# Dilated attention: splitting q and k in the tokens' layout and turning them in the transfer that turns the probabilities

## The chip, the cores and the metric

The kernel runs on one core of a Trainium2 chip. The metric is the device time of one execution in microseconds (us); of several executions the median is given. All times of rows are counted from the start of the profiled span. Engines are named as in the profile: PE (matrix multiply; PEld is its weight load), DVE (vector), ACT (scalar, activations), POOL (GpSimd), SP (the engine that here only issues transfers).

## The reference, cut to what matters

Two encoder layers over 1024 tokens of width 1024. Layer 0 mixes tokens by latent attention, layer 1 by dilated sliding-window attention in three groups; each layer ends in a squared-ReLU MLP. The change touches only the attention of layer 1:

```python
DIL_GROUPS = ((128, 1), (512, 4), (2048, 16))      # window, dilation
DIL_HEADS, DIL_HEAD_DIM = 16, 64
proj = (h @ w_in).reshape(B, S, 3, 3, 16, 64)       # group, (q k v), head, width
for gi, (window, dilation) in enumerate(DIL_GROUPS):
    q = rms_norm(proj[:, :, gi, 0], g_q[gi])
    k = rms_norm(proj[:, :, gi, 1], g_k[gi])
    v = proj[:, :, gi, 2]
    # query i sees keys i + j*dilation, |j| <= window/(2*dilation) = 64 (group 2: 64 tokens of a residue)
    s = q k^T * 64**-0.5 + bias(rel. position);  lse = logsumexp(s);  p = exp(s - lse);  o = p v
# the three groups' o are merged by softmax over their lse, then o @ w_o
```

## The kernel before

The program has two copies of the computation, one in halves (each number as a sum of two 16-bit floats, `self.half` true) and a slower one that runs only if a check of ranges fails. Only the first runs here.

The dilated stage is the method `dil`. Its work is cut into 96 steps `("qk", g, pr, tp)`: group `g` (0 to 2), pair of heads `pr` (0 to 7), and pair of 128-token tiles `tp` (0 to 3). A unit is one `(g, pr)`, four steps. Six empty steps end the stage. The loop over steps writes the instructions of several steps interleaved:

- `attend(ready, ...)` at the top: for the two query tiles `t` that are ready, `products` multiplies q with a span of 256 keys (three half products, hi*hi, lo*hi, hi*lo, and two heads that lie on the partitions 0 to 63 and 64 to 127, so 6 matmuls a tile, L2345); `scores` adds the bias and takes the maximum on DVE (L2366) and the exponential on ACT (L2372). The probabilities are split into halves `ph` (ACT L2409, then the remainder on DVE or POOL, L2410) and one transfer issued by SP turns all 128x128 blocks of `ph` into `pT` (L2411): 16 blocks a step in groups 0 and 1, 8 in group 2.
- `project` for the first and the second token tile of the step (L532 to L534, 24 matmuls of 256 columns each), which give q and k of two heads, 512 columns for 128 tokens: `psproj`.
- between the two: `stacks` for the q and k that were made two steps earlier. Four PE transposes (L2316) turn `qn`, tokens by features, into `psq`, features by tokens; ACT copies it to a half `hi` (L2321) and DVE makes the remainder `lo` (L2322). They land in `kT`, one tile of a unit with room for all 1024 keys and the q of four tiles. The tiles of this step are then `ready` for the next.
- `emit`, and `av` for the tiles whose `pT` was made by the step before: 8 matmuls a tile in groups 0 and 1, 4 in group 2 (L2424, L2425), summed by DVE (L2432).
- `qkstep` at the end, on what was just projected: squares (ACT L2295), sums (DVE L2296), the reciprocal root (ACT L132, L133, DVE L134 to L136), `qn` = projection times root (DVE L2305), and the gain on the q half (POOL L2307).

So q and k projected in step m are turned in step m+2 and used by `products` in step m+3; probabilities made in step n are used by `av` near the end of step n+1.

The PE's order is that of the program text (`pin_from`); the other engines' orders are set when the program is built, by a scheduler that lays the instructions out in modelled time. Each engine and each queue then runs in its order. SP issues, beside the turning transfers, the loads of weights (`wqkr`), of values (`vraw`), of the bias (`bt`), and the stores of `U`.

Of the kernel before, what the change touches and what calls it, by code (L numbers as in the profile page):

```python
# [9 lines left out]
F32 = mybir.dt.float32  # L10
F32R = mybir.dt.float32r
F16 = mybir.dt.float16
BF16 = mybir.dt.bfloat16
I32 = mybir.dt.int32
AF = mybir.ActivationFunctionType
ALU = mybir.AluOpType
# [4 lines left out]
P = 128  # L21
D = 1024
S = 1024
# [18 lines left out]
class K:  # L42
# [108 lines left out]
    def parts(self, hi, lo, src, scale=1.0, check=True):  # L151

        if not self.half:
            return self.split(hi, lo, src)
        nc = self.nc
        nc.scalar.activation(hi, src, AF.Copy, scale=scale)  # L156
        if not check:
            return nc.vector.scalar_tensor_tensor(lo, src, scale, hi, op0=ALU.mult, op1=ALU.subtract)
        self.nseen += 1
        assert self.nseen <= self.seen.shape[1]  # L160
        return nc.vector.scalar_tensor_tensor(lo, src, scale, hi, op0=ALU.mult, op1=ALU.subtract,  # L161
                                              accum_out=self.seen[:, self.nseen - 1 : self.nseen])
# [2028 lines left out]
    def dil(self, at0, at1, tail, wqk, vd):  # L2191


        nc, a, tc = self.nc, self.a, self.tc
# [5 lines left out]
        D_ = lambda name, shape, dt, bufs: dpool.tile(list(shape), dt, tag=name, bufs=bufs, name=self.nm(name))  # L2200
# [88 lines left out]
        def qkstep(u, tp, ps):  # L2289

            g = u["g"]
            p8 = ps.rearrange("p (n e) -> p n e", e=64)
            sq = self.T("dsq")
            ms = self.sm("dms", 8)
            nc.scalar.activation(sq, ps, AF.Square, scale=0.125)  # L2295
            nc.vector.tensor_reduce(ms, sq.rearrange("p (n e) -> p n e", e=64), op=ALU.add, axis=AX.X)  # L2296
            r = self.rstd(ms, 8, "dr", self.half)
            if self.half:
                y4 = self.sm("y4", 8)
                nc.gpsimd.tensor_tensor(y4, r, r, op=ALU.mult)  # L2300
                nc.gpsimd.tensor_tensor(y4, y4, y4, op=ALU.mult)  # L2301
                nc.gpsimd.tensor_tensor(most, most, y4, op=ALU.add)
            qn = self.T("qn")
            q8 = qn.rearrange("p (n e) -> p n e", e=64)
            nc.vector.tensor_tensor(q8, p8, r.unsqueeze(2).broadcast_to([P, 8, 64]), op=ALU.mult)  # L2305
            qq = qn.rearrange("p (i n e) -> p i n e", i=2, e=64)[:, :, 0:2, :]
            nc.gpsimd.tensor_tensor(qq, qq, gain[:, g : g + 1, :].unsqueeze(1).broadcast_to([P, 2, 2, 64]), op=ALU.mult)  # L2307
            return qn

        def stacks(u, tp, qn):  # L2310

            ps = PS("psq")
            for k in range(2):
                for i in range(2):
                    c = i * 256 + (1 - k) * P
                    nc.tensor.transpose(ps[:, (2 * k + i) * P : (2 * k + i + 1) * P], qn[:, c : c + P], self.ident)  # L2316
            s1 = 4 + tp % 2
            hi, lo = (u["k"][:, k, :].rearrange("p (s x) -> p s x", x=256)[:, tp : s1 + 1 : s1 - tp, :] for k in range(2))
            x = ps.rearrange("p (k x) -> p k x", k=2)
            if self.half:  # L2320
                nc.scalar.activation(hi, x, AF.Copy, scale=64.0)  # L2321
                nc.vector.scalar_tensor_tensor(lo, x, 64.0, hi, op0=ALU.mult, op1=ALU.subtract)  # L2322
            else:
                nc.scalar.activation(hi, x, AF.Copy)
                nc.vector.tensor_tensor(lo, x, hi.bitcast(F32), op=ALU.subtract)
            for i in range(2):
                c = S + (tp % 2 * 2 + i) * P
                u["q"][2 * tp + i] = u["k"][:, :, c : c + P]
# [7 lines left out]
        def window(g, t):  # L2336
            return t // 2 * 256 if g == 2 else min(max(P * t - 64, 0), S - 256)

        def products(u, t, pss, i):
            w0 = window(u["g"], t)  # L2340
            q = u["q"].pop(t)
            for n, (a, b) in enumerate(((0, 0), (1, 0), (0, 1))):
                for e in range(2):
                    r = slice(64 * e, 64 * e + 64)
                    nc.tensor.matmul(pss[e][:, i * 256 : (i + 1) * 256], q[r, a, :], u["k"][r, b, w0 : w0 + 256],  # L2345
                                     start=n == 0, stop=n == 2)
# [31 lines left out]
                    nc.gpsimd.memset(p[:, :, hi:256], 0)  # L2378
            return p[:, :, b0:b1]

        def attend(pairs, pe):

            pss = []
            for i, (u, t) in enumerate(pairs):
                if i % 2 == 0:
                    pss.append([PS("pss") for _ in range(2)])
                products(u, t, pss[i // 2], i % 2)
            m = [4 * P * (1 if u["g"] == 2 else 2) for u, _ in pairs]
            end = [sum(m[: i + 1]) for i in range(len(m))]
            flat = lambda x: x.rearrange("p i c -> p (i c)")[:, 0 : end[-1]]  # L2390
            parts = lambda x, i: flat(x)[:, end[i] - m[i] : end[i]].rearrange("p (k c) -> p k c", k=2)
            if pe:
                pT = D_("pT", (P, 2, 8 * P), F16, 2)
                ps = PS("pspt")
                for i, (u, t) in enumerate(pairs):
                    p = scores(u, t, pss[i // 2], i % 2)
                    for e in range(2):
                        nc.tensor.transpose(ps[:, (2 * i + e) * P : (2 * i + e + 1) * P], p[:, e], self.ident)
                n = len(pairs)
                x = ps[:, 0 : n * 2 * P].rearrange("p (i c) -> p i c", i=n)  # L2400
                y = flat(pT).rearrange("p (i k c) -> p i k c", i=n, k=2)
                nc.scalar.activation(y[:, :, 0], x, AF.Copy)
                nc.vector.tensor_tensor(y[:, :, 1], x, y[:, :, 0], op=ALU.subtract)
            else:
                ph, pT = (D_(x, (P, 2, 8 * P), F16, 2) for x in ("ph", "pT"))
                for i, (u, t) in enumerate(pairs):
                    p = scores(u, t, pss[i // 2], i % 2)
                    hi, lo = (parts(ph, i)[:, k].rearrange("p (h c) -> p h c", h=2) for k in range(2))
                    nc.scalar.activation(hi, p, AF.Copy)  # L2409
                    (nc.gpsimd if i or u["g"] == 2 else nc.vector).tensor_tensor(lo, p, hi, op=ALU.subtract)  # L2410
                nc.sync.dma_start_transpose(out=flat(pT).rearrange("p (b q) -> p b q", q=P), in_=flat(ph))  # L2411
            return [(u, t, parts(pT, i)) for i, (u, t) in enumerate(pairs)]

        def av(u, t, pT):
# [130 lines left out]
        end = max(n for n, x in enumerate(steps) if x is not None)  # L2545
# [10 lines left out]
        def fetch(n):  # L2556
            for f in wtodo.pop(n, ()):
                f()

        def fetch_split(n):  # L2560
            if n in loads:
                self.held(lambda: wts.update({firsts[n][0:3]: loads.pop(n)()}))


        vtodo, VSs = {}, {}
# [47 lines left out]
        units = {}  # L2613
        transposed, scored, ready, carry, stacking, stk, late = [], [], [], [], None, [], []
# [6 lines left out]
        for n, step in enumerate(steps):  # L2621
# [10 lines left out]
            if step is not None:  # L2632
                kind, g, pr, tp = step
                w = wts[(kind, g, pr)]
                if tp == 0:
                    units[(g, pr)] = {"g": g, "pr": pr, "q": {}, "V": VSs[(g, pr // 2)],
                                      "k": D_("kT", (P, 2, S + 512), self.DT, 2), "U": self.G("U", (P, 8, P), F32)}
                u = units[(g, pr)]
            if self.half and step is not None and tp == 0:
                bias_load(u)  # L2640
            fetch_split(n + 1)
            transposed, scored = scored, attend(ready, n > end) if ready else []
            fetch(n)
            for u_, t_, _ in scored:
                if u_["g"] == 2:
# [5 lines left out]
            if turn:  # L2651
# [3 lines left out]
                ps = ahead.pop(0)  # L2655
            elif step is not None and ahead:
                ps = ahead.pop(0)
            elif step is not None:
                ps = PS("psproj")
                project(h, w, ps, 0, 2 * tp)  # L2660
                one = True
            ready, carry = carry, []
            stk.append(stacking)
            if len(stk) > 1:
                x = stk.pop(0)
                if x is not None:
# [226 lines left out]
```

## Time and profile before

| what | value |
|---|---|
| median of 3 runs (lowest, highest) | 3010.37 us (3007.45, 3010.95) |
| the profiled execution's own time | 3005.26 us |
| its span, first to last instruction | 3003.1 us |
| the dilated stage's steps in the trace | 1548 to 2330 us |
| PE, DVE, ACT, POOL busy in the whole span | 2827.4, 2251.4, 1684.2, 922.6 us |
| granted TensorE clock, mean | 0.985 |

A group's row of the profile gives the line, the engine, the operation, what is written and read, the tile's shape and the count, then after the bar the busy time and the mean duration of one in ns, and after the second bar the engine's idle time ahead of these instructions. A row of waits gives who waited for whom, the total, the number of times and the longest. A row of a stretch gives its bounds, its length, the busy time of each engine with the number of instructions in brackets, the granted clock, the share of the 16 DMA engines and their rate. A row of the timeline gives start, duration, engine, line and operation; consecutive ones of a kind are merged (x4), and a bracket tells of idle time ahead of it and what ended it.

### The profile page before, as it was taken

The page shows a single profiled execution, that of the slowest core. Times are in us where ns is not written, and L with a number is a line of the kernel's source. Part 1 is how long each engine was busy: PE and PEld are TensorE (multiplying, and loading weights), DVE is VectorE, ACT ScalarE, POOL GpSimd, SP SyncE. Part 2 cuts the span into 40 slices and gives each one's busy share as a digit, 9 for nine tenths or more (in the row PEclk, how much of TensorE's full clock was granted, in tenths as well). Part 3 has the DMA queues.
Part 4 walks back from the last instruction along what each step waited for, and adds up shares of the span by engine and source line. Part 5 has one row for each costly group of instructions (what it writes and reads, how often), then busy time and mean ns, then how long its engine had stood idle before and what let it go on. Part 6 is the DMA issues. An engine that isn't in the chain of part 4 may idle for free. (4 is left out here: it accounts for less than half of the span.)

```text
span 3003.1 us, 54490 instructions
## 1 busy us (share of the span) xinstructions
PE 2827.4 (94%) x20148; PEld 1676.0 (56%) x20148; DVE 2251.4 (75%) x4902; ACT 1684.2 (56%) x3491; POOL 922.6 (31%) x1276
## 2 busy tenths in 40 slices
PE   6878999999999999999999989998998989999998
PEld 5634566544444444444468878876875434444443
DVE  5687777658988966788768877776886699779565
ACT  4677888825455534533238777775664355555341
POOL 6578888700211000000123344453552002110010
PEclk9999999999999999999999999999999999999999
DMA  6267455425654799546436666565656555457763
GB/s 209 72 169 161 94 117 101 131 84 188 235 188 168 251 278 289 199 159 225 171 116 148 146 139 165 145 128 117 150 129 171 144 191 210 158 186 248 238 196 86
DMA packets 589680, 503.08 MB, mean 168 GB/s; under 512 B 292277, under 2 KB 482018, under 8 KB 589402
## 3 DMA queue, kind: packets, MB, share of 16 engines
q1 hardware_dynamic: 553722, 400.74, 47.9%
q0 software_dynamic: 25248, 87.22, 7.9%
q10 hardware_dynamic: 10432, 11.54, 1.6%
q8 instruction: 159, 2.61, 0.4%
q14 instruction: 119, 0.97, 0.1%
HBM read 317.40 MB, written 125.12 MB: 147 GB/s over the span
## 5 line engine op out<-in xcount | busy, mean ns | idle before, releaser
L534 PE MATMUL psm<-hf,wf 128*128 128x512 f16 x896 | 335.8, 381 | 11.1 <-DVE wf L161 11.1
L532 PE MATMUL psm<-hf,wf 128*128 128x512 f16 x896 | 341.0, 381 | 5.0 <-ACT wf L156 5.0
L533 PE MATMUL psm<-d,d 128*128 128x512 f16 x896 | 340.8, 381 | 4.7 <-DVE d L161 4.7
L534 PE MATMUL psm<-d,d 128*128 128x512 f16 x896 | 340.7, 380 | 0.0
L533 PE MATMUL psm<-hf,wf 128*128 128x512 f16 x896 | 340.6, 380 | 0.0
L532 PE MATMUL psm<-d,d 128*128 128x512 f16 x896 | 335.0, 380 | 0.3 <-ACT d L156 0.3
L1276 POOL TENSOR_TENSOR pp<-p,pp 128x1024 f16<-128x1024 f32 x125 | 275.4, 2209 | 57.9 <-ACT pp L1269 47.8
L532 PE MATMUL psproj<-wqk,hTp 128*128 128x256 f16 x1024 | 283.0, 276 | 0.0
L533 PE MATMUL psproj<-wqk,hTp 128*128 128x256 f16 x1024 | 282.3, 276 | 0.0
L534 PE MATMUL psproj<-wqk,hTp 128*128 128x256 f16 x1024 | 282.0, 275 | 0.0
L156 ACT ACTIVATE d<-ufr 128x1024 f16<-128x1024 f32 x112 | 117.8, 1052 | 211.3 <-PE psm L534 173.3
L897 DVE TENSOR_REDUCE mx<-pmx 128x1 f32<-128x512 f32 x240 | 162.8, 687 | 78.8 <-PE pmx L895 77.4
L161 DVE SCALAR_TENSOR_TENSOR d<-ufr,d 128x1024 f16<-128x1024 f32 x112 | 136.5, 1219 | 76.5 <-ACT d L156 76.4
L1268 ACT ACTIVATE p<-pss 128x512 f32<-128x512 f32 x256 | 149.9, 590 | 43.2 <-PE pss L1259 41.8
L2372 ACT ACTIVATE pd<-pd,dnb 128x192 f32<-128x192 f32 (+2 forms) x384 | 167.3, 437 | 4.1 <-POOL y L2301 2.3
L534 PEld LDWEIGHTS <-wf 128*128 128x128 f16 x896 | 87.8, 98 | 123.3 <-DVE wf L161 19.2
L532 PEld LDWEIGHTS <-wf 128*128 128x128 f16 x896 | 87.9, 98 | 112.9 <-ACT wf L156 10.9
L534 PEld LDWEIGHTS <-d 128*128 128x128 f16 x896 | 87.9, 98 | 111.0 <-issue 6.4
L532 PEld LDWEIGHTS <-d 128*128 128x128 f16 x896 | 88.0, 98 | 106.3 <-issue 2.2
L533 PEld LDWEIGHTS <-d 128*128 128x128 f16 x896 | 87.9, 98 | 106.4 <-issue 2.5
L2410 POOL TENSOR_TENSOR ph<-pd,ph 128x512 f16<-128x512 f32 (+1 forms) x121 | 113.3, 942 | 109.3 <-ACT ph L2409 109.1
L533 PEld LDWEIGHTS <-wf 128*128 128x128 f16 x896 | 88.0, 98 | 104.9 <-issue 1.8
(439 smaller groups left out, 8122.2 us busy)
## 6 DMA issues: line engine op xcount, KB each, us to landing
ufr<-uf SPq DMA_DIRECT2D x112, 512.0 KB
w2r<-in_mlp_w SPq DMA_DIRECT2D x96, 512.0 KB
adaw<-in_ada_w SPq DMA_DIRECT2D x80, 512.0 KB
w1r<-in_mlp_w SPq DMA_DIRECT2D x64, 512.0 KB
wqkr<-in_dil_w_in SPq DMA_DIRECT2D x96, 256.0 KB
wvr<-in_dil_w_in SPq DMA_DIRECT2D x34, 512.0 KB
uf<-ub POOLq DMA_DIRECT2D x32, 512.0 KB, 3.8
uf<-ua POOLq DMA_DIRECT2D x32, 512.0 KB, 3.3
```

The lines of the kernel that those rows point to most:

```text
L156: nc.scalar.activation(hi, src, AF.Copy, scale=scale)
L161: return nc.vector.scalar_tensor_tensor(lo, src, scale, hi, op0=ALU.mult, op1=ALU.subtract, accum_out=self.seen[:, self.nseen - 1 : self.n ...
L532: mm(out, lh, rh, start=first, stop=False)
L533: mm(out, lh, rl, start=False, stop=False)
L534: mm(out, ll, rh, start=False, stop=last)
L897: nc.vector.tensor_reduce(maxes[h][:, 2 * j + b : 2 * j + b + 1], ps, op=ALU.max, axis=AX.X)
L1268: nc.scalar.activation(p[:, b * 512 : (b + 1) * 512], ps[b], AF.Exp, scale=1.0 / self.ss)
L1276: eng.tensor_tensor(q[:, 1], p, q[:, 0], op=ALU.subtract)
L2372: nc.scalar.activation(p[:, e, lo:hi], p[:, e, lo:hi], AF.Exp, scale=1.0 / self.ss, bias=nb[:, e : e + 1], accum_out=stat[:, g, t, 1, 2 * ...
L2410: (nc.gpsimd if i or u["g"] == 2 else nc.vector).tensor_tensor(lo, p, hi, op=ALU.subtract)
```

## The change

With `self.half`, q and k are split into halves before they are turned. `qkstep` multiplies by 64 on the way (what `stacks` did when it copied). One step later a new function `halves` copies `qn` to the half `hi` on ACT and makes the remainder on POOL, both into the end of the same tile `ph` that holds the probabilities' halves. The transfer of that step turns 8 more blocks: 24 in groups 0 and 1, 16 in group 2. The turned q and k stay in `pT`, which has five buffers instead of two, and `kT` is gone for them. As the keys of a unit now lie in pieces of 256 in different buffers, `products` multiplies each span of 256 keys that crosses such a border in two pieces (192 and 64 keys). Only the last two steps' q and k are still turned on PE.

```diff
-            nc.vector.tensor_tensor(q8, p8, r.unsqueeze(2).broadcast_to([P, 8, 64]), op=ALU.mult)
+            rb = r.unsqueeze(2).broadcast_to([P, 8, 64])
+            if self.half:
+                nc.vector.scalar_tensor_tensor(q8, p8, 64.0, rb, op0=ALU.mult, op1=ALU.mult)
+            else:
+                nc.vector.tensor_tensor(q8, p8, rb, op=ALU.mult)
...
+        def halves(qn, hl):
+            x = qn.rearrange("p (i s c) -> p s i c", i=2, s=2)
+            hl = hl.rearrange("p (a i c) -> p a i c", a=4, i=2)
+            nc.scalar.activation(hl[:, 0:3:2], x, AF.Copy)
+            nc.gpsimd.tensor_tensor(hl[:, 1:4:2], x, hl[:, 0:3:2], op=ALU.subtract)
+
         def stacks(u, tp, qn):
+            if qn is None:
+                return
             ps = PS("psq")
...
+            if self.half:
+                x = ps.rearrange("p (k x) -> p k x", k=2)
+                kq = u["kq"][tp] = D_("kT", (P, 4, 256), F16, 2)
+                nc.scalar.activation(kq[:, 0:3:2], x, AF.Copy)
+                nc.vector.tensor_tensor(kq[:, 1:4:2], x, kq[:, 0:3:2], op=ALU.subtract)
+                return
...
         def products(u, t, pss, i):
             w0 = window(u["g"], t)
+            if self.half:
+                kq = u["kq"]
+                q = kq[t // 2][:, 0:2, t % 2 * P : t % 2 * P + P]
+                n1 = 256 - w0 % 256
+                ks = [(0, kq[w0 // 256][:, 2:4, w0 % 256 : 256])]
+                if n1 < 256:
+                    ks.append((n1, kq[w0 // 256 + 1][:, 2:4, 0 : 256 - n1]))
+                for o, x in ks:
+                    for n, (a, b) in enumerate(((0, 0), (1, 0), (0, 1))):
+                        for e in range(2):
+                            r = slice(64 * e, 64 * e + 64)
+                            nc.tensor.matmul(pss[e][:, i * 256 + o : i * 256 + o + x.shape[2]], q[r, a, :], x[r, b, :],
+                                             start=n == 0, stop=n == 2)
+                return
...
-        def attend(pairs, pe):
+        def attend(pairs, pe, extra=None):
...
+            hl = 8 * P if extra is not None else 0
+            pTs = lambda: (D_("pT", (P, 24 * P), F16, 5) if self.half else ...)
...
-                ph, pT = (D_(x, (P, 2, 8 * P), F16, 2) for x in ("ph", "pT"))
+                ph = D_("ph", (P, 24 * P if self.half else 16 * P), F16, 2)
+                pT = pTs()
...
-                nc.sync.dma_start_transpose(out=flat(pT).rearrange("p (b q) -> p b q", q=P), in_=flat(ph))
+                n = (end or [0])[-1]
+                if hl:
+                    u, tp, qn = extra
+                    halves(qn, ph[:, n : n + hl])
+                    u["kq"][tp] = pT[:, n : n + hl].rearrange("p (a x) -> p a x", a=4)
+                nc.sync.dma_start_transpose(out=pT[:, 0 : n + hl].rearrange("p (b q) -> p b q", q=P), in_=ph[:, 0 : n + hl])
...
-            transposed, scored = scored, attend(ready, n > end) if ready else []
+            extra = stacking if self.half and n < end else None
+            transposed, scored = scored, attend(ready, n > end, extra) if ready or extra else []
+            if extra:
+                stacking = stacking[:2] + (None,)
```

More of the change, by code (lines that the diff above doesn't have):

```diff
@@ L2314, in stacks @@
                 for i in range(2):
-                    c = i * 256 + (1 - k) * P
+                    c = i * 256 + (k if self.half else 1 - k) * P
                     nc.tensor.transpose(ps[:, (2 * k + i) * P : (2 * k + i + 1) * P], qn[:, c : c + P], self.ident)
+            if self.half:
[4 more added lines that the diff above has]
+                return
             s1 = 4 + tp % 2
@@ L2319, in stacks @@
             x = ps.rearrange("p (k x) -> p k x", k=2)
[L2320 to L2325, printed above, removed]
+            nc.scalar.activation(hi, x, AF.Copy)
+            nc.vector.tensor_tensor(lo, x, hi.bitcast(F32), op=ALU.subtract)
             for i in range(2):
@@ L2387, in attend @@
                 products(u, t, pss[i // 2], i % 2)
+            hl = 8 * P if extra is not None else 0
+            pTs = lambda: (D_("pT", (P, 24 * P), F16, 5) if self.half else D_("pT", (P, 2, 8 * P), F16, 2).rearrange("p i c -> p (i c)"))
             m = [4 * P * (1 if u["g"] == 2 else 2) for u, _ in pairs]
             end = [sum(m[: i + 1]) for i in range(len(m))]
-            flat = lambda x: x.rearrange("p i c -> p (i c)")[:, 0 : end[-1]]
+            flat = lambda x: x[:, 0 : (end or [0])[-1]]
             parts = lambda x, i: flat(x)[:, end[i] - m[i] : end[i]].rearrange("p (k c) -> p k c", k=2)
             if pe:
-                pT = D_("pT", (P, 2, 8 * P), F16, 2)
+                pT = pTs()
                 ps = PS("pspt")
@@ L2404, in attend @@
             else:
-                ph, pT = (D_(x, (P, 2, 8 * P), F16, 2) for x in ("ph", "pT"))
+                ph = D_("ph", (P, 24 * P if self.half else 16 * P), F16, 2)
+                pT = pTs()
                 for i, (u, t) in enumerate(pairs):
@@ L2635, in dil @@
                 if tp == 0:
-                    units[(g, pr)] = {"g": g, "pr": pr, "q": {}, "V": VSs[(g, pr // 2)],
-                                      "k": D_("kT", (P, 2, S + 512), self.DT, 2), "U": self.G("U", (P, 8, P), F32)}
+                    units[(g, pr)] = {"g": g, "pr": pr, "q": {}, "kq": {}, "V": VSs[(g, pr // 2)],
+                                      "k": None if self.half else D_("kT", (P, 2, S + 512), self.DT, 2), "U": self.G("U", (P, 8, P), F32)}
                 u = units[(g, pr)]
```

## The prediction

> **What bounds the kernel now.** I read the busy time by stretch first, then the groups of the dilated stage, PE's waits in it, and the timeline of a few steps. The stretches come first (length, then PE, PEld, DVE, ACT, POOL busy, clock, DMA share, rate):
>
> ```profile
> 1600.00:1700.00 100.00, 99.03 (x1098) 86.09 (x1097) 81.14 (x266) 78.49 (x230) 38.63 (x78) 1.00 0.66 155
> 2065.00:2290.00 225.00, 195.72 (x1975) 167.39 (x1976) 182.66 (x593) 139.45 (x477) 111.40 (x185) 0.97 0.64 143
> 1548.00:2330.00 782.00, 721.12 (x7487) 610.13 (x7485) 601.18 (x1977) 547.59 (x1698) 325.96 (x641) 0.98 0.61 141
> ```
>
> Group 0 (first row) is bound by PE. In group 2 (second row) PE has 29 us of holes and DVE is busy 81%. Over the stage PE lacks 61 us of full. PE's waits:
>
> ```profile
> PE psav L2424 <- DMA pT<-ph: 25.0, 12, 6.2
> PE pss L2345 <- DVE kT L2322: 14.8, 12, 2.8
> PE pss L2345 <- ACT kT L2321: 7.8, 10, 1.8
> PE psq L2316 <- POOL qn L2307: 5.8, 1, 5.8
> PE psq L2316 <- DVE qn L2305: 2.9, 2, 2.4
> ```
>
> The last four, 31.3 us, are waits on the path that the change takes out (qn to PE, kT to the products). The first, 25.0 us, is on the transfer that the change makes longer. The groups that the change touches, in the stage:
>
> ```profile
> L2409 ACT ACTIVATE ph<-pd 128x512 f16<-128x512 f32 x128 | 77.2, 616 | 0.2
> L2410 POOL TENSOR_TENSOR ph<-pd,ph 128x512 f16<-128x512 f32 x63 | 74.1, 1176 | 90.3 <-ACT ph L2409 90.2
> L2322 DVE SCALAR_TENSOR_TENSOR kT<-psq,kT 128x512 f16<-128x512 f32 x96 | 65.9, 686 | 37.7 <-ACT kT L2321 37.7
> L2305 DVE TENSOR_TENSOR qn<-psproj,dry 128x512 f32<-128x512 f32 x95 | 65.4, 688 | 2.2
> L2316 PE MATMUL psq<-ident,qn 128*128 128x128 f32 x384 | 59.3, 276 | 8.8 <-POOL qn L2307 5.8 <-DVE qn L2305 2.9
> L2321 ACT ACTIVATE kT<-psq 128x512 f16<-128x512 f32 x96 | 55.3, 576 | 10.4 <-PE psq L2316 10.4
> L2411 SPq DMA_TRANSPOSE pT<-ph x93: 1232/1599/4400, 1559.2 to 2290.4; - x93
> ```
>
> And the rows of three steps, in order of time (products of one step at 1601.34, of the next at 1608.57: a step of 7.23 us):
>
> ```profile
> 1600.99 0.22 PE L2424 MATMUL psav<-vs,pT 128*128 128x128 f16 x1
> 1601.05 0.19 PE L2425 MATMUL psav<-vs,pT 128*128 128x64 f16 x1
> 1601.08 0.22 PE L2424 MATMUL psav<-vs,pT 128*128 128x128 f16 x1
> 1601.34 0.83 PE L2345 MATMUL pss<-kT 64*128 64x256 f16 x12
> 1601.96 1.60 SPq L2411 DMA_TRANSPOSE pT<-ph  x1
> 1604.73 0.60 PE L2316 MATMUL psq<-ident,qn 128*128 128x128 f32 x4
> 1605.17 0.27 PE L532 MATMUL psproj<-wqk,hT 128*128 128x256 f16 x1
> 1605.69 0.73 POOL L2307 TENSOR_TENSOR qn<-qn,dgain 128x256 f32<-128x256 f32 x1
> 1607.79 0.22 PE L2424 MATMUL psav<-vs,pT 128*128 128x128 f16 x1
> 1608.55 1.16 POOL L2410 TENSOR_TENSOR ph<-pd,ph 128x512 f16<-128x512 f32 x1 [2.13 <-ACT ph L2409]
> 1608.57 0.39 PE L2345 MATMUL pss<-kT 64*128 64x256 f16 x4
> 1609.73 1.57 SPq L2411 DMA_TRANSPOSE pT<-ph  x1
> 1615.09 0.10 PEld L2424 LDWEIGHTS <-pT 128*128 128x128 f16 x1 [0.20 <-DMA pT<-ph]
> 1617.19 4.04 SPq L2411 DMA_TRANSPOSE pT<-ph  x1
> 1623.31 0.23 PE L2424 MATMUL psav<-vs,pT 128*128 128x128 f16 x1 [0.82 <-DMA pT<-ph]
> 2008.25 1.60 SPq L2411 DMA_TRANSPOSE pT<-ph  x1
> 2011.94 0.29 PE L2424 MATMUL psav<-vs,pT 128*128 128x128 f16 x1 [2.71 <-DMA pT<-ph]
> ```
>
> These rows hold the main point. The transfer issued at 1609.73 carries the probabilities of the products at 1601.34 (its last input is POOL's remainder, which ends at 1609.71) and is used at 1615.09. In the quiet case (2008.25 to 2011.94) 16 blocks are there 3.69 us after the issue. So the transfer of 1601.96, used at 1607.79, has 5.83 - 3.69 = 2.14 us to spare. Behind loads the same transfer takes longer: 5.36 us from 1609.73, with PE's weight load just held up by it, and 6.12 us from 1617.19, with PE standing. PE waits so at 12 of the 93 transfers, one step in eight.
>
> **The change, part by part.**
>
> *PE's transposes go* in 94 of 96 steps. One costs not its 276 ns but its place in PE's stream: the four that start at 1604.73 put off the next projection to 1605.17, so 0.44 us a step, 94 x 0.44 = **-41 us** of PE time.
>
> *Spans in two pieces.* In groups 0 and 1, six of the eight tiles of a unit cross a border of 256 keys: 16 units x 6 = 96 tiles, three pairs of matmuls each, so 288 pairs of 64 keys more, and as many pairs of 256 made 192. The columns stay the same, hence the lower end is 0. The upper end is a full pair's place, 0.109 us (four transposes' 0.44 us is 0.109 each, and a tile's three pairs of products have about the same pitch: 0.83 us for 12 with the last one's drain): 31 us. The nearest row is the 64-column matmul of `av`: from 1600.99 to 1601.08 PE does one matmul of 128 and one of 64 columns, with two weight loads, in 0.085 us. A pair of 64 then costs two short places (a third of 0.085 each), some 0.057 us, less the 64 of 256 columns saved (0.027): 0.03 x 288 = **+8 us**. The page TensorE: Matmul & The Clock Gate of the Trainium skill, section LDWEIGHTS, states that a weight load takes its columns divided by 1.2 in ns, 107 ns for 128, whatever the rows; by that an estimate for the 288 pairs is 31 us, too. The 0.085 us for two loads disagrees, as these loads overlap matmuls.
>
> *ACT:* a copy of 128x512 from SBUF instead of PSUM, 616 for 576 ns: +4 us on an engine idle for 234 of 782 us; nothing.
>
> *DVE:* L2322 goes, 94 x 0.686 = 64 us less. L2305 becomes the kind of operation that L2322 is, 686 for 688 ns: nothing.
>
> *POOL:* a remainder of 128x512 more a step, 94 x 1.176 = 111 us, so 326 becomes 437 of 782 us. Load is no matter; order is. qn is ready when POOL's gain ends, 1606.42. Ahead of POOL's remainder at 1608.55 lies 2.1 us of idle time: ACT's copy (0.62) and POOL's remainder (1.18) just fit, and the transfer is issued as before. If the order puts them last, it is issued up to 0.62 + 1.18 = 1.8 us later. Ends 0 and 1.8; I take 0.4, as it fits here, but on the margin. What waits behind it on SP are the loads of weights, values and bias: they are for steps ahead, and are put off by the same time and by a longer issue (8 blocks took 1232 ns at least, 16 take 1599, so about 2.0).
>
> *The transfer.* Its data, by the rate while it runs alone:
>
> ```profile
> 1609.73:1610.73 1.00, 1.00 (x11) 0.90 (x10) 1.00 (x7) 0.92 (x3) 0.67 (x3) 1.00 0.00 0
> 1610.73:1612.60 1.87, 1.87 (x19) 1.72 (x18) 1.87 (x9) 1.87 (x5) 0.00 (x0) 1.00 1.10 252
> ```
>
> Nothing moves in the first microsecond, then 252 GB/s with the DMA engines full. 8 blocks are 262 KB: 1.04 us more for every transfer (two short ones more at the start). The turned q and k themselves are needed by the products two steps later, after `av` of the same transfer: no wait of their own.
>
> **Landing, the disputed term.** The transfer lands 1.04 + 0.4 = 1.44 us later, while PE, faster by 0.44 us a step, asks for it 2 x 0.44 earlier counted from its products. An ordinary step's 2.14 us become -0.2, just in time. The 12 steps that wait now wait 1.44 + 0.44 = 1.88 more each: 23 us. As many neighbours like the one at 1615.09, with nothing to spare, would wait the same; half of it, as a wait ahead of them gives them time: 11 us. The ordinary ones, 0.1 to 0.2 us in some 50 steps: 8 us. Together **+42 us**. Lower end: the 1.04 us alone, at 12 waits, 12 us. Upper end, issue 1.8 us later: (1.04 + 1.8 + 0.44) x 12 = 39, half as much for the neighbours, 20, and in some 40 ordinary steps of groups 0 and 1 (2.14 - 1.04 - 1.8 - 0.88 = -1.6, 0.8 a step as two steps share it, half of this since a wait gives time to the next) 16: 75 us.
>
> **The four waits that go:** 31 us at most. In those steps ACT and DVE were late with kT since they were behind with other work, and they now make the transfer's inputs; I keep a third as later landing: **-22 us**.
>
> Sum: -41 + 8 + 42 - 22 = **-13 us**. The profiled execution took 3005.26 us (span 3003.1), 5.1 below the median of 3010.37. Its gain is carried over to the median: 2997.
>
> **Rivals.**
>
> (a) *The transfer keeps its time.* POOL's idle stretch takes the remainder everywhere and DVE, freed of 0.69 us a step, delivers earlier: landing at its lower end, all four waits gone: -41 + 8 + 12 - 31 = -52, 2958. For it: POOL's 2.1 us of idle time. Against: waits of 12 steps with nothing to spare.
>
> (b) *The landing sets the step: slower.* POOL's remainder comes last, the transfer is issued 1.8 us later, landing 75: -41 + 8 + 75 - 22 = +20, 3030. It decides once the landing is later by more than the 2.14 us of an ordinary step. For it: POOL's operations get longer beside DVE's:
>
> ```profile
> 1604.90 0.20 POOL L2300 TENSOR_TENSOR y<-dry 128x8 f32<-128x8 f32 x1 [2.71 <-DVE dry L136]
> 1612.82 1.22 DVE L161 SCALAR_TENSOR_TENSOR wqk<-wqkr,wqk 128x1024 f16<-128x1024 f32 x1
> 1613.05 1.05 POOL L2300 TENSOR_TENSOR y<-dry 128x8 f32<-128x8 f32 x1 [2.60 <-DVE dry L136]
> ```
>
> The same small product takes 0.20 us alone and 1.05 beside DVE's L161, ending with it; the remainder, moved from DVE to POOL, is exposed to this for 1.18 us a step. The page SBUF — State Buffer of the Trainium skill states (Practical consequences) that a DVE instruction with two SBUF inputs and a POOL instruction that reads SBUF shut each other out for a whole instruction. These rows agree; by that rule the moved work can hold up DVE, too, which the sum leaves out.
>
> (c) *The pieces cost full pairs:* 31 instead of 8, +10, 3020, slower. Against it stands the 0.085 us.
>
> (d) *PE's time was cover.* Transposes gone, the steps stay as long as engines and transfers make them, and waits take up what PE saves: within 6 us of 3010. For it: an ordinary step's balance comes out at -0.2 us, so little is left either way.
>
> **How the numbers follow.** A difference of 0.2%, 6 us, is about what a measurement of this kernel can tell from none. The forecast (2980 to 3004 by its own) has 0.40, (a) 0.14, (b) 0.25, (c) 0.07, (d) 0.14. The forecast's upper end gives 0.04 to no change, and (d) leans a little to slower. Faster 0.50, same 0.17, slower 0.33. The range of 8 in 10 goes from (a) to just over (b): 2957 to 3034.
>
> **What the profile of the changed kernel would show.** L2316's successor with 8 matmuls instead of 384, and projections following each other with no 0.44 us between: PE's share right. 1728 products instead of 1152; the stage's DVE at about 540 us, POOL at about 437. A transfer's issue near 2.0 us at the median, quiet landing near 4.7. PE's waits on kT gone, on the transfer 25 becoming about 67 us. If these waits stay under 40, (a) holds; if they pass 90 and steps of group 0 are longer than 7.23 us, (b). If pairs of 64 keys stand 0.1 us apart, (c). The prediction is wrong above all if POOL's remainder stands behind that of the probabilities in most steps, or if the order of the other engines, laid out anew, moves work that I left in place.

## The result

The change made the kernel slower: 3074.93 us at the median (3072.85 to 3075.54, four runs) against 3008.91, a ratio of 1.0218 [1.02, 1.0236]. Forecast was 2997, with a range up to 3034. The profiled execution's span went from 3003.1 to 3073.6 us. All of it lies in the dilated stage, where the last store of group 0's and of group 1's results and the last merge of group 2 mark the end of each group. Of the kernel before (line, engine, operation, count, shortest/median/longest ns, first and last start):

```profile
L2448 SPq DMA_DIRECT2D U<-U x8: 364/522/791, 1596.8 to 1812.6; - x8
L2452 SPq DMA_DIRECT2D U<-U x16: 534/558/608, 1835.3 to 2071.7; - x16
L2503 DVE TENSOR_TENSOR U<-U,um x32: 675/692/1505, 2088.9 to 2336.0; 128x512 f32<-128x512 f32 x32
```

and of the changed one:

```profile
L2485 SPq DMA_DIRECT2D U<-U x8: 359/366/372, 1599.0 to 1844.4; - x8
L2489 SPq DMA_DIRECT2D U<-U x16: 529/552/607, 1867.2 to 2116.6; - x16
L2540 DVE TENSOR_TENSOR U<-U,um x32: 678/691/1431, 2133.4 to 2407.3; 128x512 f32<-128x512 f32 x32
```

Group 0 ends 31.8 us later, group 1 44.9, group 2 71.3, so the groups by themselves lost 31.8, 13.1 and 26.4 us and none escaped. From group 0's first store to its last, 28 steps, a step took 7.71 us before and takes 8.76.

The stage by stretches, in the profile after (columns as in the prediction; the second row is the part by which the stage is longer):

```profile
1548.00:2330.00 782.00, 662.10 (x7287) 555.78 (x7285) 520.20 (x1742) 517.76 (x1597) 407.82 (x704) 0.93 0.72 157
2330.00:2410.00 80.00, 65.76 (x457) 39.23 (x456) 54.55 (x158) 32.80 (x102) 21.71 (x33) 0.89 0.71 184
```

PE, busy 721 us of the first 782 before, is busy 662, and no engine is nearer to full than that. The clock granted to it fell from 0.98 to 0.93. What PE waits for (total, times, longest), over the stage:

```profile
PE psav L2461 <- DMA pT<-ph: 122.9, 49, 6.7
PE psot L2557 <- DVE U L2540: 5.0, 3, 1.7
PE psy L532 <- DVE qn L2307: 2.7, 1, 2.7
```

The waits on kT and on qn's transposes are gone, and the one on the transfer is 123 us instead of 25, at 49 transfers instead of 12. The groups that answer to those shown before, and the transfers:

```profile
L2319 POOL TENSOR_TENSOR ph<-qn,ph 128x512 f16<-128x512 f32 x94 | 112.3, 1194 | 50.6 <-ACT ph L2318 49.8
L2318 ACT ACTIVATE ph<-qn 128x512 f16<-128x512 f32 x94 | 58.3, 620 | 28.3 <-POOL qn L2311 27.6
L2367 PE MATMUL pss<-pT 64*128 64x256 f16 x552 | 46.3, 309 | 0.1
L2367 PE MATMUL pss<-pT 64*128 64x192 f16 x576 | 43.4, 260 | 0.0
L2367 PE MATMUL pss<-pT,pT 64*128 64x64 f16 x576 | 17.5, 197 | 0.0
L2367 PE MATMUL pss<-kT 64*128 64x256 f16 x24 | 1.7, 271 | 0.0
L2329 PE MATMUL psq<-ident,qn 128*128 128x128 f32 x8 | 1.5, 272 | 0.0
L2448 SPq DMA_TRANSPOSE pT<-ph x95: 1232/3097/6789, 1550.4 to 2359.9; - x95
```

There are 8 transposes and 1728 products, as foreseen; a transfer's issue holds SP for 3.10 us at the median, not for 2.0.

How one step goes wrong shows at the end of group 0 (timeline; in brackets the idle time of the engine before the instruction and its cause), with the stretches around it below:

```profile
1782.49 1.16 POOL L2442 TENSOR_TENSOR ph<-pd,ph 128x512 f16<-128x512 f32 x1
1782.59 0.61 ACT L2318 ACTIVATE ph<-qn 128x512 f16<-128x512 f32 x1
1783.62 0.27 PE L532 MATMUL psproj<-wqk,hs 128*128 128x256 f16 x1
1783.88 1.16 POOL L2319 TENSOR_TENSOR ph<-qn,ph 128x512 f16<-128x512 f32 x1
1785.06 8.90 SPq L2448 DMA_TRANSPOSE pT<-ph  x2
1790.61 0.29 PE L2461 MATMUL psav<-vs,pT 128*128 128x128 f16 x1 [6.17 <-DMA pT<-ph]
```

```profile
1784.40:1790.60 6.20, 0.04 (x1) 0.00 (x0) 4.61 (x10) 3.08 (x9) 4.40 (x9) 0.75 0.56 128
1790.60:1794.00 3.40, 3.39 (x31) 2.42 (x32) 1.24 (x5) 0.63 (x1) 2.27 (x5) 0.50 0.79 112
1797.00:1800.00 3.00, 3.00 (x41) 2.71 (x40) 1.08 (x3) 1.53 (x3) 1.19 (x1) 1.00 0.01 3
```

POOL makes the probabilities' remainder (ending 1783.65), then that of q and k (ending 1785.04), and only then the transfer is issued. It is used 5.55 us later; PE has stood 6.17 us. In the 3.4 us that follow, PE is granted half its clock, and later full clock again: the hole is paid for twice. The Trainium skill, page TensorE: Matmul & The Clock Gate, section Why this matters for your kernels, advises against idle gaps of PE over some 3 us between bursts of matmuls, as the clock then falls to half; the 0.50 behind this hole of 6.17 us agrees.

In group 2 a step goes wrong in another way, about once a unit (rows of one step):

```profile
2146.86 0.67 POOL L2442 TENSOR_TENSOR ph<-pd,ph 128x256 f16<-128x256 f32 x1
2148.25 0.63 ACT L2318 ACTIVATE ph<-qn 128x512 f16<-128x512 f32 x1 [0.57 <-POOL qn L2311]
2148.25 0.58 ACTq L2572 DMA_DIRECT2D um<-U  x1
2148.96 1.15 POOL L2319 TENSOR_TENSOR ph<-qn,ph 128x512 f16<-128x512 f32 x1 [0.58 <-ACT ph L2318]
2150.14 4.55 SPq L2448 DMA_TRANSPOSE pT<-ph  x1
2162.42 0.29 PE L2461 MATMUL psav<-vs,pT 128*128 128x128 f16 x1 [6.02 <-DMA pT<-ph]
```

The probabilities' halves are ready at 2147.53. The transfer goes out 2.6 us later, as it waits for q: POOL's gain, ACT's copy, POOL's remainder. It is then among the loads of the first groups' outputs (`um`, 256 KB each, four a unit, two of them issued in the 2 us ahead of it and two in the 2.1 us behind), and PE uses it 12.3 us after its issue.

### The profile page after: what moved, and what is told of

It is laid out like the page before. It is cut to its first block, busy times and chain, and to the rows that moved or that the text cites. A ratio compares the mean times of both kernels' runs of the same rounds, so it can differ in the third digit from the quotient of the medians.

```text
span 3073.6 us, 54788 instructions
## 1 busy us (share of the span) xinstructions
PE 2825.0 (92%) x20348; PEld 1658.0 (54%) x20348; DVE 2216.2 (72%) x4808; ACT 1686.2 (55%) x3491; POOL 1024.7 (33%) x1370
## 5 line engine op out<-in xcount | busy, mean ns | idle before, releaser
L532 PE MATMUL psproj<-wqk,hTp 128*128 128x256 f16 x1024 | 287.1, 280 | 0.0
L533 PE MATMUL psproj<-wqk,hTp 128*128 128x256 f16 x1024 | 286.2, 280 | 0.8 <-DVE wqk L161 0.7
L534 PE MATMUL psproj<-wqk,hTp 128*128 128x256 f16 x1024 | 285.7, 279 | 0.0
L2461 PE MATMUL psav<-vs,pT 128*128 128x128 f16 x640 | 75.0, 232 | 123.0 <-DMA pT<-ph 122.9
L2469 DVE TENSOR_REDUCE U<-psav 128x128 f32<-128x256 f32 x192 | 76.3, 418 | 152.2 <-PE psav L2462 152.1
L534 PEld LDWEIGHTS <-wf 128*128 128x128 f16 x896 | 87.7, 98 | 122.1 <-DVE wf L161 18.2
L271 DVE SCALAR_TENSOR_TENSOR adacc<-adaw,cond,adacc 128x1024 f32<-128x1024 f32 (+1 forms) x98 | 129.1, 1318 | 30.9 <-DMA adaw<-in_ada_w 30.1
L532 PEld LDWEIGHTS <-wf 128*128 128x128 f16 x896 | 87.8, 98 | 114.3 <-ACT wf L156 11.3
L534 PEld LDWEIGHTS <-d 128*128 128x128 f16 x896 | 87.9, 98 | 111.0 <-issue 6.4
L533 PEld LDWEIGHTS <-d 128*128 128x128 f16 x896 | 87.9, 98 | 106.5 <-issue 2.5
```

Source lines behind the costliest of these rows:

```text
L271: return self.nc.vector.scalar_tensor_tensor(acc, w, c, acc, op0=ALU.mult, op1=ALU.add)
L532: mm(out, lh, rh, start=first, stop=False)
L533: mm(out, lh, rl, start=False, stop=False)
L534: mm(out, ll, rh, start=False, stop=last)
L2461: nc.tensor.matmul(o, pT[:, 0, c], v, start=b == 0, stop=False)
L2469: nc.vector.tensor_reduce(u["U"][:, t, :].rearrange("p (e d) -> p e d", e=2), ps[:, 0 : 128 * k].rearrange("p (e k d) -> p e d k", e=2, k= ...
```

## The experiments

All ratios are to the kernel before, timed on the same chip. Group ends are from the same three rows as above, against the kernel before.

**e1_sep.** The changed kernel, with q's and k's halves in tiles and a transfer of 8 blocks of their own, so that the probabilities' transfer is as short as before.

```
-  halves(qn, ph[:, n : n + hl])
-  nc.sync.dma_start_transpose(out=pT[:, 0 : n + hl]..., in_=ph[:, 0 : n + hl])
+  nc.sync.dma_start_transpose(out=pT[:, 0:n]..., in_=ph[:, 0:n])
+  qh, kq = D_("qh", (P, 8 * P), F16, 2), D_("kq", (P, 8 * P), F16, 5)
+  halves(qn, qh)
+  nc.sync.dma_start_transpose(out=kq..., in_=qh)
```

> The changed kernel, but the halves of q and k go into a tile of their own and are turned by a second transfer of 8 blocks, issued after that of the probabilities, which is back at 16 blocks and waits for nothing of q and k. Theory 1 (the probabilities' transfer lands too late for PE, as it carries 8 more blocks and waits for POOL's remainder of q and k; PE's holes then halve the clock): PE's waits on the probabilities' transfer fall from 123 us to under 50, the half-clock stretches go, and the time comes to 2960 to 3000 us. Theory 2 (it is the load: 8 more blocks a step on the DMA engines and SP, 111 us more on POOL): the load is the same, so the time stays above 3045.

Measured: 3028.24 us, 1.0071 [1.0054, 1.0087], between the two theories' times. Of the 66 us, 42 go when the two transfers are parted; 24 stay. PE's waits:

```profile
PE psav L2464 <- DMA pT<-ph: 54.9, 36, 4.8
PE pss L2367 <- DMA kq<-qh: 44.7, 14, 10.4
```

By the group ends, groups 0 and 1 together cost 2.4 us (the last store of group 1 starts at 2074.1), and group 2 27.6 (the last merge at 2366.0). So the 24 us lie in group 2, and of the second wait, up to 10.4 us, nearly all. There q's and k's transfers of 8 blocks landed 10.8 to 13.8 us after their issue once in four of the eight units, among the loads of the first groups' outputs, and 2.7 us after it when they were alone.

**e2_len and e5_len2.** The kernel before, with 8 more blocks in each transfer that nobody reads: the length alone. In e2_len a POOL memset fills them each step; in e5_len2 two fixed tiles hold the zeros.

```
-  nc.sync.dma_start_transpose(out=flat(pT)..., in_=flat(ph))
+  n = end[-1] + (8 * P if self.half else 0)
+  nc.sync.dma_start_transpose(out=pT[:, 0:n]..., in_=ph[:, 0:n])
```

> The kernel before, with 8 blocks of zeros (set by POOL at the start of the step) at the end of each turning transfer: 24 and 16 blocks as in the change, but no wait for q and k, and q and k still turned on PE. If the transfer's length is the main part of theory 1, the time is 3045 or more; if the wait for POOL's remainder is, then under 3030, with PE's waits on the transfer between 30 and 60 us. Theory 2 (load on the DMA engines and SP) expects 3045 or more, too, and then e1 tells them apart.

> Again the kernel before with 8 blocks more in each turning transfer, without the flaw of e2, where POOL's clearing waited for the transfer two steps back (250 us of POOL's waits) and held up its other work: here the probabilities' halves lie in two fixed tiles, cleared once, and the 8 further blocks are zeros, or in group 2 old probabilities, that nobody reads. Theory 1 (length): the transfer lands 0.9 to 1.4 us later at the median, PE's waits on it grow from 25 to 50 to 70 us, the clock loses some 10 us more, and the time is 3035 to 3055. If POOL's wait made most of e2: under 3020.

Measured: e2_len 3062.19, 1.0186 [1.0166, 1.0206]; e5_len2 3027.58, 1.0064 [1.0043, 1.0086]. The first says nothing of the length, since the memset brought a wait of its own; POOL's waits show it, with the second run's PE below:

```profile
POOL ph L2407 <- DMA pT<-ph: 250.4, 83, 7.6
```

```profile
PE psav L2436 <- DMA pT<-ph: 47.3, 27, 7.7
PE pss L2345 <- DVE kT L2322: 16.1, 10, 5.1
```

By e5_len2 8 blocks more cost 20 us with all else in place, which lies between its expectations: waits on the transfer went from 25.0 to 47.3. By the group ends (last store of group 1 2099.3, last merge 2359.6) groups 0 and 1 take 27.6 us more, and group 2 takes 4.0 less.

**e3_pieces.** The kernel before, with each span that crosses a border of 256 keys in two pieces.

```
+  n1 = 256 - w0 % 256
+  for o, m in ((0, n1), (n1, 256 - n1)) if self.half and n1 < 256 else ((0, 256),):
```

> The kernel before, with the spans of keys that cross a border of 256 multiplied in two pieces. From the changed kernel's trace (24 matmuls of a step with two pieces take 0.776 us to the next projection, 12 take 0.762): no change, 3007 to 3012. The prediction's 8 us would give 3017, its rival of full pairs 3040.

Measured: 3004.75, 1.0003 [0.9992, 1.0013]. The pieces cost nothing that can be measured.

**e4_two.** The kernel before, with two of four transposes a step left out (keys stand in for queries, so what is computed differs).

```
-  for k in range(2):
+  for k in range(1 if self.half else 2):
```

> The kernel before with two of the four PE transposes of a step left out; the copies read the first two blocks twice, so k is a copy of q's block and the output isn't the reference's. 96 x 0.22 = 21 us of PE time less, and nothing else. If a step is bound by PE: 2988. If PE's time was cover for engines and transfers (the prediction's rival d): 3000 or more, with the waits of PE on the transfer grown by as much as the transposes gave.

Measured: 2990.23, 0.9945 [0.9924, 0.9965]: half of the transposes are worth 14 us of time, where their place in the stream is 21 us. Of PE's saving, two thirds reach the end, between the two expectations. The waits on the transfer grow from 25.0 to 30.3 us, those on kT from 22.6 to 25.7.

**e6_dve, e7_sepdve, e8_first.** Three attempts on POOL's order: q's and k's remainder on DVE in the changed kernel, the same in e1_sep, and the changed kernel with the halves called ahead of the scores in the program's text.

```
-  nc.gpsimd.tensor_tensor(hl[:, 1:4:2], x, hl[:, 0:3:2], op=ALU.subtract)
+  nc.vector.tensor_tensor(hl[:, 1:4:2], x, hl[:, 0:3:2], op=ALU.subtract)
```

> The changed kernel with the remainder of q and k made by DVE instead of POOL; still one transfer of 24 blocks. Theory 1 with POOL's order as its second part: the transfer is issued 0.5 to 1.2 us earlier than in the changed kernel, and the time falls to 3035 to 3055. If the length alone matters: 3065 to 3080, as in the changed kernel.

> e1's two transfers with the remainder of q and k on DVE. In e1 PE waited 45 us for q and k, up to 10 us at a unit's start in group 2, where POOL was busy with merging; on DVE, which has the time of the removed remainder free, this wait should fall below 15 us and the time to 2970 to 3000, under the kernel before: PE's transposes are then gained and the probabilities' transfer is as before. If the load of 8 more blocks a step on DMA engines and SP is what counts, it stays at 3015 to 3035.

> The changed kernel with the call of halves moved ahead of the scores in the program text, so that in the orders of ACT and POOL q and k come ahead of the probabilities where they are ready. If POOL's order is what makes the transfer late: issue 0.5 to 1.1 us earlier in steps where q is ready in time, 3040 to 3060. If the length is: 3065 to 3080. It can also be worse, as ACT then holds the probabilities up for q and k.

Measured: 3071.39, 1.0213 [1.0196, 1.023]; 3036.55, 1.0108 [1.009, 1.0125]; 3072.33, 1.0227 [1.0207, 1.0246]. Against 1.0218 and e1_sep's 1.0071 nothing is won, and the expected gains all missed. In the changed kernel the remainder of q and k is the transfer's last input at 55 of 93 transfers (12 of 32 in group 0, 19 of 32 in group 1, 24 of 29 in group 2). Made by DVE it is still the last at 62, and the transfer is issued little sooner if at all (9.2, 8.6 and 10.3 us after the products in groups 0, 1 and 2, at the median, against 9.0, 8.8 and 10.6). e8_first says nothing about the order: the other engines' orders are set by the scheduler, and q's and k's remainder is last at 54 transfers instead of 55.

**e9_early and e12_early2.** Still one joined transfer, but q and k in it are those of the step before, so they are ready a step ahead of it; their products come one step later. In e9_early the values' halves are made one step later, too; in e12_early2 they are not.

```
-  extra = stacking if self.half and n < end else None
+  extra = stk[-1] if self.half and stk and stk[-1] and n <= end else None
-  if len(stk) > 1:
+  if len(stk) > 2:
```

> The changed kernel, still one transfer of 24 blocks, but the q and k that ride in it are those of the step before: they are ready a whole step ahead of the transfer, and their products come one step later (the values' halves are made one step later, too). Theory 1 (the joined transfer waits for q's and k's chain of projection, norm, copy and remainder, so the probabilities land late): the transfer then only has its length against it. The kernel before with transfers of 24 blocks took 3028; with half of PE's transposes left out it gained 14, so with all of them some 28: expected 2995 to 3015, PE's waits on the probabilities' transfer under 60 us instead of 123, the stage's clock over 0.95. Rival (the length does it: 3.1 us of issue and the load on the DMA engines): it stays within 15 us of the changed kernel's 3073, waits on the transfer over 100.

> The run with q and k of the step before in the joined transfer (3041), with the values' halves at their old place. Theory (its 20 us of waits on the weights' halves came from the values, the rest of what was lost is the length of 24 blocks, worth 20 us, against which PE's missing transposes stand): no waits on the weights' halves, 3015 to 3026, of which about 7 are the one step more at the end. Rival (these waits come from the later products, or others take their place): within 6 us of 3041.

Measured: 3040.58, 1.012 [1.0103, 1.0137], and 3035.77, 1.0097 [1.008, 1.0114]. PE's waits in the first, and the main one in the second:

```profile
PE psav L2461 <- DMA pT<-ph: 82.8, 36, 7.4
PE psproj L533 <- DVE wqk L161: 13.0, 9, 2.6
PE psproj L532 <- ACT wqk L156: 7.7, 6, 1.6
```

```profile
PE psav L2461 <- DMA pT<-ph: 103.9, 42, 7.3
```

Having q and k ready gives back 32 and 35 us of the 66, at the price of a step more at the stage's end. That is less than theory 1 asked for and more than its rival. The waits on the weights' halves went with the values, as supposed, but waits on the transfer took their place, and the time moved 5 us: the rival held in the second run. The transfer is still late, even with q and k ready.

**e10_later and e13_later2.** Two transfers, the products of q and k one step later, which gives their transfer a step more; the values' halves one step later in e10_later, in their old place in e13_later2.

```
-  if len(stk) > 1:
+  if len(stk) > 2:
```

> Two transfers (as in the run with q's and k's halves in a transfer of their own, 3028), with the products of q and k one step later, so that their transfer of 8 blocks has a step more to land (the values' halves one step later, too). Theory 2 (in group 2, once a unit, turned q and k stand in the queues behind the loads of the first two groups' outputs, and PE waits up to 10 us for them): PE's waits on that transfer go from 44.7 us to under 8, holes in group 2 from 57 to about 35 us, time 2990 to 3010. Rival (PE then waits for the probabilities or the other engines instead; q's and k's transfer was only the last of several): waits on the probabilities' transfer rise above 80 and the time stays 3020 to 3035.

> The run with two transfers and q's and k's products one step later (3030), with the values' halves at their old place. Theory 2 (late turned q and k in group 2 cost the 24 us that two transfers lost): waits on the weights' halves gone, those on q's and k's transfer stay near 0, time 3003 to 3014. Rival (others take their place): 3024 to 3032.

Measured: 3029.71, 1.0072 [1.0055, 1.0089], and 3024.73, 1.0066 [1.0049, 1.0082]: no better than e1_sep's 1.0071. The wait on q's and k's transfer is off the list in both, and the other is longer:

```profile
PE psav L2464 <- DMA pT<-ph: 70.4, 26, 8.2
```

```profile
PE psav L2464 <- DMA pT<-ph: 85.4, 29, 8.0
```

For the time as a whole the rival held, though in e10_later the waits on the probabilities' transfer stayed under its 80. By the group ends of e13_later2 (last store of group 1 2086.3, last merge 2360.1) group 2 takes 9.5 us more than before instead of 27.6, so late q and k were two thirds of its loss; groups 0 and 1 take 14.6 more instead of 2.4, about 7 of it the step that was added (an estimate from the 7.23 us of a step before).

**e11_g2pe and e14_g2pe_later.** Two transfers in groups 0 and 1; in group 2 q and k are turned on PE as before. In e14_g2pe_later the products also come one step later.

```
-  extra = stacking if self.half and n < end else None
+  extra = stacking if self.half and stacking and stacking[0]["g"] < 2 else None
```

> Two transfers in groups 0 and 1, and in group 2 q and k turned on PE as before. Theory 2: group 2 takes what it took before, and groups 0 and 1 are within 5 us of the kernel before (transposes gone against longer waits): 3000 to 3012 us. Rival (the loss of 24 us with two transfers lies evenly in all three groups): 3018 to 3024.

> Two transfers in groups 0 and 1, group 2 turned on PE (3001), and the products of q and k one step later in all groups, the values' halves at their old place. In groups 0 and 1 PE's waits on q's and k's transfer were only 2.3 us, so a step more has little to give there; in group 2 the waits on the halves of q and k were 12, on the gain 6, which it can hide. Theory: 2993 to 3003, a step more at the end (7 us) against up to 18 us. Rival (the waits on the probabilities' transfer, 59 us, grow by what goes): 3005 to 3012.

Measured: 3001.37, 0.9984 [0.9975, 0.9994], and 3012.11, 1.0025 [1.0014, 1.0036]. In the first, theory 2 held:

```profile
L2492 SPq DMA_DIRECT2D U<-U x16: 531/548/1472, 1844.6 to 2070.7; - x16
L2543 DVE TENSOR_TENSOR U<-U,um x32: 676/691/1504, 2084.4 to 2331.5; 128x512 f32<-128x512 f32 x32
```

```profile
PE psav L2464 <- DMA pT<-ph: 59.1, 33, 6.6
PE pss L2367 <- DMA kq<-qh: 2.3, 5, 1.1
```

Group 2 is back at its time (260.8 us from the last store to the last merge, 264.3 before), and groups 0 and 1 end 1.0 us earlier. Of the versions that compute the same, it is the one that beats both kernels, by 0.16%, less than the 0.2% that the prediction took as the least that can be told. In the second both expectations missed: 3012.11 lies at the rival's upper end, but its waits on the transfer grew by 5 us only, to 64.3. By the same estimate the step added at the end accounts for about 7 of the 11 us between the two; the rest is open.

## Why the prediction was wrong

Each step's delays can be read from the trace, in groups 0, 1 and 2: how long after a step's products its transfer is issued (median), how long after the issue it has landed (mean), and how long before PE's use that is (median; 0.05 us is a transfer for which PE stood waiting). They are worked out over all transfers of a run, the products of each step with the transfer that carries their probabilities, in the order of the program. The last two columns are from the group ends.

| kernel | products to issue, us | landing, us | to spare, us | PE's waits on it, us | groups 0 and 1, us | group 2, us |
|---|---|---|---|---|---|---|
| before | 8.0 / 7.8 / 8.7 | 4.3 / 4.4 / 4.0 | 1.9 / 2.4 / 2.8 | 25.0 | | |
| e5_len2 (longer) | 8.0 / 7.8 / 8.3 | 5.4 / 5.6 / 5.1 | 0.8 / 1.4 / 2.0 | 47.3 | +27.6 | -4.0 |
| e1_sep (two transfers) | 9.2 / 8.8 / 8.8 | 4.5 / 4.6 / 4.0 | 0.05 / 0.05 / 3.5 | 54.9 | +2.4 | +27.6 |
| changed | 9.0 / 8.8 / 10.6 | 5.8 / 5.5 / 5.7 | 0.05 / 0.05 / 0.05 | 122.9 | +44.9 | +26.4 |
| e12_early2 (q, k ready) | 8.7 / 8.6 / 8.8 | 5.5 / 5.8 / 5.2 | 0.1 / 0.05 / 1.7 | 103.9 | +27.1 | +7.8 |

The length alone adds 1.1 to 1.2 us to the landing and nothing to the issue; two transfers add 1.0 to 1.2 us to the issue in groups 0 and 1 and little to the landing. The changed kernel has both, 2.3 us together in groups 0 and 1 and 3.5 in group 2, and PE without transposes asks 0.88 sooner. The prediction's 2.14 us to spare was a fair reading of an ordinary step: the median over all 93 is 2.25. It is used up: before, 18 of 93 transfers had less than 0.3 us to spare, in the changed kernel 60. No run has the later issue alone, and the runs differ in PE's transposes (in e5_len2 they are still there), so how the 66 us divide between issue and length isn't shown.

- **Transposes gone, -41: right for PE, too large for the time.** PE does 8 instead of 384. By e4_two two thirds of such a saving reach the end, an estimate of some 28 us for all of it.
- **Pieces, +8: too large.** e3_pieces measured 1 us, within its uncertainty of none. Rival (c) is out.
- **DVE and ACT at nothing: right as work.** L2307 takes 690 ns, ACT's copy 620. POOL's remainder takes 1194 ns in the new place against 1176, so the rule that the prediction took from the Trainium skill (page SBUF — State Buffer, section Practical consequences: a DVE instruction with two SBUF inputs contends with a POOL instruction that reads SBUF) shows no price in these means. POOL is busy 408 us in the first 782 and 430 in the stage's 862, against the forecast 437.
- **Issue later by 0.4: too small.** Measured at the median: 1.0 us in groups 0 and 1, 1.9 in group 2. On average the transfer goes out 0.8, 1.3 and 2.3 us after the probabilities' last half is made (0.1 to 0.3 before), which is its wait for q and k. POOL's remainder of q and k is last at 55 of 93 transfers, in most steps, the sign by which the prediction called itself wrong. In e12_early2 that wait is gone (0.1 to 0.3 us again) and the issue is still 0.6 to 0.8 us later in groups 0 and 1. In e1_sep SP issues q's and k's transfer first at some steps, and the probabilities' goes out 0.5 and 0.7 us after its last input in groups 0 and 1. The rest of the lateness in these two isn't settled; PE, without transposes, does its products sooner, and the engines that make the transfer's inputs may not follow.
- **Landing, 1.04 for 8 blocks: nearly right, +1.1 to +1.2 by e5_len2.** But SP's hold of 2.0 us was 3.1, and the changed kernel's landing is +1.1 to +1.6.
- **Landing's sum, +42: the step that failed.** It held 1.44 + 0.88 against 2.14, so the ordinary step came out at -0.2, and 50 of them were priced at 0.1 to 0.2 us. With the 2.3 us that groups 0 and 1 show (1.0 at the issue, 1.3 at the landing) it is 3.2 against 2.14, 1.1 us too late in an ordinary step: measured, PE waits at 49 of 95 transfers, and 98 us more instead of 42. The upper end of 75 was too low as well: it halved the neighbours' lateness and took a quarter of that of the ordinary steps.
- **A term is missing: the clock.** PE's holes, counted over the stage (1548 to 2337 us before, to 2408 after), grew from 61 to 134 us. The half clock was granted for 31 us of the stage before and for 129 us of the changed one; counting half of PE's busy time in these stretches as lost, that is 13 and 51 us. So -41 for the transposes, +1 for the pieces, +73 for the holes and +38 for slower matmuls make +71, and the stage is 71 us longer. The +38 is read from the clock's records and was not tried by a run of its own. The prediction read the clock's column and priced no hole beyond its length.
- **Four waits gone, -22 of 31:** they are gone from the list as forecast. What they were worth in time can't be told from the growth of the other.
- **Rival (b)** is what happened: waits over 90 us, steps of group 0 over 7.23 us (8.76 on average; before they took 7.71, so that sign was set too low), POOL's remainder last in most steps. Its point of decision, later by more than 2.14 us, was met on average in groups 0 and 1 (2.3) and in group 2 (3.5); its price of +20 was a third of the true one.

Not foreseen at all was group 2, which the prediction didn't add up by itself. The length alone costs nothing there (e5_len2, -4.0), while late q and k cost 26 to 28 us, joined or not: joined, they hold the probabilities back (2.3 us on average) until the transfer falls among the loads of the first groups' outputs and lands 9 to 12 us after its issue, six times in eight units; in a transfer of their own they land late behind the same loads. A step more for q and k gives back most of it (e12_early2 +7.8, e13_later2 +9.5), and turned on PE it is gone (e11_g2pe). That it is these loads was read from their times and not tried by moving them.

Open remains why q and k ready a step ahead (e12_early2) leave 104 us of waits on the joined transfer, where the length alone (e5_len2) has 47, with PE's transposes in place. In groups 0 and 1 the two lose the same, 27 us, though the one has PE's transposes gone, against a step more.

## What to carry to other kernels

Before moving work onto a transfer that an engine already waits for, add up all delays of that transfer (longer issue, more data, later inputs, and the engine's own saving, which makes it ask sooner) and hold the sum against the slack of an ordinary step, not only against the steps that wait today; two delays that each seem to fit can fail together. A hole of PE costs its length and, when it is long, slower matmuls behind it, so price it twice (here 73 us of holes and, by the clock's records, 38 us of slower matmuls). And look at each stage for itself: with a transfer of its own, the same move cost 2 us in two groups and 28 in the third.

## What the hardware showed

The issue of a transposing transfer is not proportional to its blocks: in the kernel before 1232 ns at the least (8 blocks) and 1599 at the median (mostly 16), in the changed one 3097 at the median (mostly 24). A transfer of 8 blocks landed 2.7 us after its issue when it was alone, and 10.8 to 13.8 us after it among loads of 1 MB. Products of 64x64 in 576 further matmuls cost nothing that could be measured (1.0003). And PE's granted clock was 0.50 in the 3.4 us right behind a hole of 6.17 us.
